# Neighbourhood attention on one core: 48 groups of four column blocks in three steps, with the weighted values of a group in one run

## The chip, the core and the metric

The kernel runs on one NeuronCore of a Trainium2 chip. A time is device microseconds of one execution of the whole program. Five engines have a part here: TensorE (PE in the profile, its weight loads PEld), VectorE (DVE), ScalarE (ACT), GpSimd (POOL) and SyncE (SP), which issues every DMA of the program on one queue. Each engine takes its instructions in the order in which they were written into its stream.

## What is computed

One layer of an encoder runs over 16 meta tokens, a batch of 512 tokens (p) and one of 1024 tokens (a and b, 512 each), all with the same weights, in float32. The input is normalised and projected to seven parts of 1024 columns: two for a gated convolution of width 31 and its gate, three for attention (q, k, v) and one for its gate. Attention has 16 heads of 64 and looks at a window of the token grid around each query. Cut to what matters here:

```
s = einsum('bjqhd,brjkhd->bhjqrk', q_r, k_blk) + bias + mask_add
s_meta = einsum('bjqhd,bmhd->bhjqm', q_r, k_meta_s)
p = softmax(concatenate([s, s_meta], axis=-1), axis=-1)
o = einsum('bhjqrk,brjkhd->bjqhd', p_grid, v_blk) + einsum('bhjqm,bmhd->bjqhd', p_meta, v_meta)
mixed = concatenate([conv_out, att * silu(a_gate)], axis=-1)
y = h + rms_norm(einsum('ble,ed->bld', mixed, w_out))
```

## The kernel before

A projection is made of 24 matmuls into one PSUM bank (`mm`, line 133): eight slices of the contraction, and for each the product of the rounded weights with the rounded input and two correction products with the rest of the weights (`wlo`) or of the input. The program runs in three stages. First come the norm and the convolution (on DVE), with projections of the gates and of v beside it; then attention; then the gated product with the output weights (`py`, line 682), for 12 tiles of 128 tokens.

Attention goes over 8 pairs of heads (`p`) and, for each, 3 ranges of the grid (`g`), which share one k projection (`pair_proj`, four projections) and have one q projection each (`pair_q`). A range has 8 column blocks of 64 queries. One column block takes these steps:

- scores: 3 matmuls into a bank of pool `ps_s`, which has two banks (`ss`, line 548);
- softmax: DVE adds the bias table and takes the maximum (line 556), ACT the exponential (559), DVE scales by the reciprocal of the sum (561); the tile is `pt`;
- transposes: 2 or 3 on PE into a bank of `ps_t`, which has two banks too (`tp`, line 564), and ACT copies them to `pT` (566);
- weighted values: 4 or 6 matmuls with 64 columns of weights (`po`, line 571). The two heads of a pair write partitions 0 to 63 and 64 to 127 of one bank, so these matmuls use half the columns of the array each; every other matmul of this stage uses all 128. The trace holds two records for each of these instructions.

After 8 column blocks DVE copies the bank out (`mo`, line 574), and SP writes it to memory (`mad`, 575). Nothing in the code says how these steps interleave: a list scheduler orders each engine's stream. It takes what is written first in the code before what is written later, where both are ready by its own estimate of times, and fills with later work where not. So the projections that are written for the next range or pair become fill between the steps of the current one.

At the end of attention the first tile of the output stage (`mix(0)`) is queued, on ACT, behind the last exponential. The output weights (`load_wo`, lines 616 to 627) are loaded by SP, rounded by ACT and split by DVE.

Of the kernel before, what the change touches and what calls it, by code (L numbers as in the profile page):

```python
# [53 lines left out]
VPB = 1  # L54

# [12 lines left out]
def tile_encoder(ctx: ExitStack, tc: tile.TileContext, mt, xn, w_main, w_v, wo, cw, cb, lg, lb, pg, postg, rbt, rmask, y):  # L68
# [25 lines left out]
    msq = const.tile([128, 128], F32, name="msq")  # L94
# [368 lines left out]

    def pair_proj(p):
# [3 lines left out]
        kl = pool.tile([128, 8, NROW, 8], F32R, name="kl")  # L468
        for (c0, c1) in MGROUPS:
# [34 lines left out]
    def pair_q(p, wqh, wql, g):  # L504
        ps = ps_mm.tile([128, 512], F32, name="mm", tag="mm")
        proj(ps, wqh, wql, 16 + g * 512, 16 + g * 512 + 512)
        res = []
        for hf in range(2):
# [8 lines left out]
            res.append((qh, ql))  # L517
        return res

    def attention(p, g, kh, kl, qs):  # L520
        G = GR[g]
        R = G["R"]
        R8 = R * 8
        esl = slice(p * 128, p * 128 + 128)
        if g == 0:
# [3 lines left out]
        else:  # L529
            vt = apool.tile([104, 8, 128], F32, name="vt", bufs=2)  # L530
            nc.sync.dma_start(vt[:R8], vd[:, G["vrow"] * 8:G["vrow"] * 8 + R8, esl].rearrange("b k e -> k b e"))
        po = ps_o.tile([128, 8, 64], F32, name="po")
        for j in range(8):
            qh, ql = qs[j // 4]
            jj = j % 4
            e = ebufs[g][{0: 1, 7: 2}.get(j, 0)]
            if g == 0:
                b0, nk, key = min(max(j - 1, 0), 5), 3, "k3"
            elif j in (0, 7):
                b0, nk, key = min(j, 6), 2, "k2"  # L540
            else:
                b0, nk, key = j - 1, 3, "k3"
            nt, kt = (2, 108) if g == 0 else (nk, R8)
            ra, rn, ro = G[key]
            w = rn * 8
            ss = ps_s.tile([128, 512], F32, name="ss")
            for i, (q, k) in enumerate(((qh, kh), (qh, kl), (ql, kh))):
                nc.tensor.matmul(ss[:, :nk * w], lhsT=q[:, jj].rearrange("p h x -> p (h x)"),  # L548
                                 rhs=k[:, b0:b0 + nk, ra:ra + rn, :].rearrange("p b r c -> p b (r c)"),
                                 start=(i == 0), stop=(i == 2))  # L550
# [3 lines left out]
            pv3 = pv.rearrange("p (k x) -> p k x", k=nk)  # L554
            sm = apool.tile([128, 4], F32, name="sm", bufs=4)
            nc.vector.tensor_tensor_reduce(out=pv3, in0=sv_, in1=e.rearrange("p k r c -> p k (r c)"), scale=1.0,  # L556
# [4 lines left out]
            nc.vector.tensor_scalar(out=pv, in0=pv, scalar1=sm[:, 3:4], scalar2=None, op0=ALU.mult)  # L561
            tp = ps_t.tile([128, 512], F32, name="tp")
# [3 lines left out]
            nc.scalar.copy(out=pT[:kt, :nt * 128], in_=tp[:kt, :nt * 128])  # L566
            for k in range(nt):
                for h in range(2):
                    hs = slice(h * 64, h * 64 + 64)
                    v = vt[:, k, b0, hs] if g == 0 else vt[:R8, b0 + k, hs]  # L570
                    nc.tensor.matmul(po[hs, j, :], lhsT=v, rhs=pT[:kt, k * 128 + h * 64:k * 128 + h * 64 + 64],  # L571
                                     start=(k == 0), stop=(k == nt - 1))
        mo = apool.tile([128, 512], F32, name="mo", bufs=2)
        nc.vector.tensor_copy(out=mo, in_=po.rearrange("p j x -> p (j x)"))
        nc.sync.dma_start(mad[g][p], mo)

    for p in range(NPAIR):
        e_build(p)
        kh, kl = pair_proj(p)
        wqh, wql = load_w(24 + p)  # L580
        for g in range(3):
            qs = pair_q(p, wqh, wql, g)
            attention(p, g, kh, kl, qs)
        if p >= NAG1:
            for _ in a_gate(p):
                pass
    for cs in [(c,) for c in range(NCG1, 6)] + [(6, 7)]:
        for _ in c_gate(cs):
            pass
# [192 lines left out]
```

## Time and profile before

| | before |
|---|---|
| time, median of 3 runs | 1517.15 us (1515.48 to 1517.2) |
| the profiled execution, its own time | 1517.83 us |
| its span, first to last instruction | 1516.1 us |
| around the span (1517.83 - 1516.1) | 1.73 us |
| PE busy | 1460.5 us (96%) |
| DVE, ACT, POOL busy | 1006.9, 585.3, 351.4 us |
| granted TensorE clock, mean | 0.986 |
| first scores to the last matmul of weighted values (starts) | 725.9 to 1234.8 us |

PE's busy time counts each matmul from its start to its end, and matmuls of a stream overlap, so it doesn't say how densely they follow one another. What a matmul costs the stream is the distance from its start to the start of the next one, read from the timeline. In the timeline, equal instructions that follow one another are one row, with a count (x16) and the length from the first start to the last end.

### The profile page before, as it was taken

The page shows a single profiled execution, that of the slowest core. Times are in us where ns is not written, and L with a number is a line of the kernel's source. Part 1 is how long each engine was busy: PE and PEld are TensorE (multiplying, and loading weights), DVE is VectorE, ACT ScalarE, POOL GpSimd, SP SyncE. Part 2 cuts the span into 40 slices and gives each one's busy share as a digit, 9 for nine tenths or more (in the row PEclk, how much of TensorE's full clock was granted, in tenths as well). Part 3 has the DMA queues.
Part 4 walks back from the last instruction along what each step waited for, and adds up shares of the span by engine and source line. Part 5 has one row for each costly group of instructions (what it writes and reads, how often), then busy time and mean ns, then how long its engine had stood idle before and what let it go on. Part 6 is the DMA issues. An engine that isn't in the chain of part 4 may idle for free.

```text
span 1516.1 us, 24156 instructions
## 1 busy us (share of the span) xinstructions
PE 1460.5 (96%) x9506; PEld 1241.3 (82%) x9506; DVE 1006.9 (66%) x1739; ACT 585.3 (39%) x1296; POOL 351.4 (23%) x258
## 2 busy tenths in 40 slices
PE   7998999999999898969999999999999979999998
PEld 6987898989988787757888888888887867888876
DVE  7699989797959698991545545546555557553442
ACT  7312121122111121112544545545544567456652
POOL 1133232233031323562121111111210002122121
PEclk9999999999999999989999999999999999999999
DMA  8013123141122131024112222212222367454542
GB/s 274 24 49 104 46 59 112 53 137 61 48 74 90 38 103 63 29 87 122 52 56 65 63 61 82 66 44 61 86 58 81 119 189 218 131 169 131 148 137 75
DMA packets 124470, 138.91 MB, mean 92 GB/s; under 512 B 8110, under 2 KB 96430, under 8 KB 124356
## 3 DMA queue, kind: packets, MB, share of 16 engines
q1 hardware_dynamic: 124356, 137.36, 29.6%
q8 instruction: 75, 1.23, 0.3%
q14 instruction: 39, 0.32, 0.1%
HBM read 99.05 MB, written 42.71 MB: 94 GB/s over the span
## 4 chain that ended last, share of the span: by engine, by line
PE 76%; DVE 9%; DMA 6%; issue 4%; POOL 2%; ACT 2%; SPq 0%; DVEq 0%; POOLq 0%; ACTq 0%
PE mm L133 49%; PE mm L286 8%; DVE z L223 5%; PE ss L548 5%; PE po L571 5%; PE tp L564 4%; PE py L682 4%; DMA mb<-std 2%; DMA mx<-zs 2%; POOL wlo L116 1%; POOL ml L655 1%; DMA yo<-in_wo 1%; DVE mx L653 1%; DVE mx L649 1%; DVE mx L648 1%
## 5 line engine op out<-in xcount | busy, mean ns | idle before, releaser
L133 PE MATMUL mm<-uw,whi 128*128 128x512 f32 (+2 forms) x2688 | 757.2, 364 | 3.2 <-ACT whi L115 3.2
L133 PEld LDWEIGHTS mm<-uw,whi 128*128 128x128 f32 x2688 | 485.1, 190 | 83.7 <-ACT whi L115 4.9
L223 DVE SCALAR_TENSOR_TENSOR z<-ub,cw_sb,z 128x1536 f32<-128x1536 f32 (+2 forms) x300 | 507.7, 1710 | 23.4 <-ACT z L221 15.2
L133 PE MATMUL mm<-uw,wlo 128*128 128x512 f32 (+2 forms) x1344 | 488.4, 364 | 18.1 <-POOL wlo L116 18.1
L133 PEld LDWEIGHTS mm<-uw,wlo 128*128 128x128 f32 x1344 | 255.6, 190 | 56.8 <-POOL wlo L116 19.1
L116 POOL TENSOR_TENSOR wlo<-wraw,whi 128x1024 fp32r<-128x1024 f32 x48 | 150.0, 3126 | 437.9 <-ACT whi L115 433.0
L682 PE MATMUL py<-uw,mh 128*128 128x512 f32 x576 | 180.0, 394 | 6.8 <-ACT mh L654 6.2
L286 PE MATMUL mm<-vh,uw 128*128 128x256 f32 x768 | 141.9, 284 | 1.1 <-ACT uw L158 0.6
L566 ACT COPY pT<-tp 108x256 f32<-108x256 f32 (+4 forms) x192 | 76.1, 425 | 153.4 <-PE tp L564 146.9
L682 PEld LDWEIGHTS py<-uw,mh 128*128 128x128 f32 x576 | 108.8, 189 | 31.1 <-ACT mh L654 6.4
L286 PEld LDWEIGHTS mm<-vh,uw 128*128 128x128 f32 x768 | 119.4, 190 | 3.3 <-ACT uw L158 1.0
L559 ACT ACTIVATE pt<-pt,sm 128x216 f32<-128x216 f32 (+4 forms) x192 | 96.9, 505 | 46.3 <-DVE sm L558 44.6
L682 PE MATMUL py<-uw,ml 128*128 128x512 f32 x288 | 113.2, 394 | 0.8 <-POOL ml L655 0.8
L556 DVE CUSTOM_DVE_ANT_0 pt<-ss,ei 128x216 f32<-128x216 f32 (+2 forms) x144 | 60.8, 439 | 77.7 <-PE ss L548 73.7
L655 POOL TENSOR_TENSOR ml<-mx,mh 128x1024 fp32r<-128x1024 f32 x22 | 54.4, 2490 | 245.5 <-ACT mh L654 245.5
L286 PE MATMUL mm<-vl,uw 128*128 128x256 f32 x384 | 108.1, 282 | 0.0
L561 DVE TENSOR_SCALAR pt<-pt,sm 128x216 f32<-128x216 f32 (+4 forms) x192 | 76.2, 397 | 5.5
L564 PE MATMUL tp<-ident,pt 128*96 128x128 f32 (+2 forms) x480 | 78.8, 282 | 0.0
L286 PEld LDWEIGHTS mm<-vl,uw 128*128 128x128 f32 x384 | 72.7, 189 | 0.8 <-issue 0.5
L115 ACT CAST whi<-wraw 128x1024 fp32r<-128x1024 f32 x48 | 50.3, 1048 | 48.9 <-PE mm L133 32.8
L571 PEld LDWEIGHTS po<-pT,vt 96*64 96x64 f32 (+1 forms) x1408 | 47.8, 137 | 23.5 <-issue 13.4
L682 PEld LDWEIGHTS py<-uw,ml 128*128 128x128 f32 x288 | 54.4, 189 | 13.6 <-POOL ml L655 1.3
(147 smaller groups left out, 1630.7 us busy)
## 6 DMA issues: line engine op xcount, KB each, us to landing
wraw<-in_w_main SPq DMA_DIRECT2D x48, 512.0 KB
xt<-in_xn SPq DMA_DIRECT2D x12, 512.0 KB
vd<-vs SPq DMA_DIRECT2D x96, 64.0 KB
zs<-zc SPq DMA_DIRECT2D x24, 256.0 KB
cgd<-ag SPq DMA_DIRECT2D x24, 256.0 KB
agd<-ag SPq DMA_DIRECT2D x24, 256.0 KB
mad<-mo SPq DMA_DIRECT2D x24, 256.0 KB
mx<-zs SPq DMA_DIRECT2D x12, 512.0 KB
```

The source lines that it names most:

```text
L116: eng.tensor_tensor(out=lo, in0=raw, in1=hi.bitcast(F32), op=ALU.subtract)
L133: nc.tensor.matmul(ps[:, :n], lhsT=w[:, dc, :], rhs=u[dc // 4][:, dc % 4, :], start=(dc == 0 and i == 0), stop=(dc == DC - 1 and i == 2))
L223: nc.vector.scalar_tensor_tensor(out=zv, in0=ub[:, a:b, k:k + 512], scalar=cw_sb[:, c, k:k + 1], in1=zv, op0=ALU.mult, op1=ALU.add)
L286: nc.tensor.matmul(ps[:, :256], lhsT=u[dc // 4][:, dc % 4, :], rhs=w[dc // 4][:, dc % 4, :], start=(dc == 0 and i == 0), stop=(dc == DC - ...
L548: nc.tensor.matmul(ss[:, :nk * w], lhsT=q[:, jj].rearrange("p h x -> p (h x)"), rhs=k[:, b0:b0 + nk, ra:ra + rn, :].rearrange("p b r c -> ...
L559: last[0] = nc.scalar.activation(out=pv, in_=pv, func=AF.Exp, bias=sm[:, 1:2], scale=1.0, accum_out=sm[:, 2:3])
L561: nc.vector.tensor_scalar(out=pv, in0=pv, scalar1=sm[:, 3:4], scalar2=None, op0=ALU.mult)
L564: nc.tensor.transpose(out=tp[:kt, k * 128:k * 128 + 128], in_=pv[:, k * kt:k * kt + kt], identity=ident)
L566: nc.scalar.copy(out=pT[:kt, :nt * 128], in_=tp[:kt, :nt * 128])
L571: nc.tensor.matmul(po[hs, j, :], lhsT=v, rhs=pT[:kt, k * 128 + h * 64:k * 128 + h * 64 + 64], start=(k == 0), stop=(k == nt - 1))
L655: (nc.vector if t < MLT else nc.gpsimd).tensor_tensor(out=ml, in0=mx, in1=mh.bitcast(F32), op=ALU.subtract)
L682: nc.tensor.matmul(pss[hf], lhsT=m[e // 8][:, e % 8], rhs=w[e][:, hf * 512:hf * 512 + 512], start=(e == 0 and i == 0), stop=(e == 15 and i ...
```

## The change

The steps of a column block are written apart, for groups of four column blocks: 8 pairs x 3 ranges x 2 halves make 48 groups. Step n of the loop writes the scores and softmax of group n, the weighted values of group n-2, the transposes of group n-1 and one unit of projections, in this order. The weighted values are queued on PE behind the last score matmul written so far (`issue_after`), and thereby stand together. There are now 6 `pt` tiles, 4 `pT` tiles, one `mo` tile and 2 `raw` tiles (3, 2, 2 and 3 before). The work of the last groups is followed by what is left of the gate projections, as before.

```diff
...
+PTB, PTTB = 6, 4
...
     def pair_proj(p):
...
+        kbufs[p] = kh, kl
...
-        return kh, kl
+            yield
...
-            raw = apool.tile([128, 15, 24], F32, name="raw", bufs=3)
+            raw = apool.tile([128, 15, 24], F32, name="raw", bufs=2)
...
+    def scores(p, g, hf):
+        if hf == 0:
+            load_values(p, g)
+        kh, kl = kbufs[p]
+        qh, ql = qbuf.pop((p, g, hf))
+        R8 = GR[g]["R"] * 8
+        for jj in range(4):
...
-            pt = apool.tile([128, 312], F32, name="pt", bufs=3)
+            pt = apool.tile([128, 312], F32, name="pt", bufs=PTB)
...
+    def transposes(p, g, hf):
+        for j in range(hf * 4, hf * 4 + 4):
...
             for k in range(nt):
                 nc.tensor.transpose(out=tp[:kt, k * 128:k * 128 + 128], in_=pv[:, k * kt:k * kt + kt], identity=ident)
-            pT = apool.tile([108, 384], F32, name="pT", bufs=2)
+            pT = apool.tile([108, 384], F32, name="pT", bufs=PTTB)
             nc.scalar.copy(out=pT[:kt, :nt * 128], in_=tp[:kt, :nt * 128])
...
+    def weighted(p, g, hf):
+        if hf == 0:
+            pos[p, g] = ps_o.tile([128, 8, 64], F32, name="po")
+        po, vt = pos[p, g], vts[p, g]
+        for j in range(hf * 4, hf * 4 + 4):
...
+    def between(p, i):
+
+        if i in (0, 2):
+            pair_q(p, i // 2 + 1)
+        elif p == NPAIR - 1:
+            next(rest, None)
+        elif i == 5:
+            pair_q(p + 1, 0)
+        else:
+            if i == 1:
+                knext[0] = pair_proj(p + 1)
+                next(knext[0])
+            next(knext[0])
...
+    groups = [(p, g, hf) for p in range(NPAIR) for g in range(3) for hf in range(2)]
+    for n in range(len(groups) + 2):
+        if n < len(groups):
+            p, g, hf = groups[n]
+            if (g, hf) == (0, 0) and p > 0:
+                e_build(p)
+            scores(p, g, hf)
+        else:
+            next(rest, None)
+        if n >= 2:
+            with tc.issue_after(last_qk[0].ins):
+                weighted(*groups[n - 2])
+        if 0 <= n - 1 < len(groups):
+            transposes(*groups[n - 1])
+        if n < len(groups):
+            between(p, g * 2 + hf)
```

What the scheduler makes of it, engine by engine, is read from the two built programs; lines 564, 586 and 602 of the changed kernel are the scores, transposes and weighted values. First PE in the middle of a pair, a range's last weighted values before the change:

```order
L133 MATMUL mm<-uw,whi 128x512 x2
L571 MATMUL po<-pT,vp 64x64 x8
L564 MATMUL tp<-ident,pt 108x128 x4
L548 MATMUL ss<-kh,qh_5536 128x264
L548 MATMUL ss<-kl,qh_5536 128x264
L548 MATMUL ss<-kh,ql_5537 128x264
```

PE at such a place after the change:

```order
L133 MATMUL mm<-uw,whi 128x512 x2
L586 MATMUL tp<-ident,pt 108x128 x2
L564 MATMUL ss<-kh,qh_5535 128x264
L564 MATMUL ss<-kl,qh_5535 128x264
L564 MATMUL ss<-kh,ql_5536 128x264
L602 MATMUL po<-pT,vt 64x64 x22
L564 MATMUL ss<-kh,qh_5541 128x256
```

The weighted values of two column blocks stood between projections and transposes; those of four now stand between scores, and the transposes stand apart from them in twos and threes. Over the whole stage, counted in the two orders, the 960 weighted-value instructions make 120 runs before and 50 after; behind a run stand transposes 107 times before (33 after), scores 10 times (16) and others 3 times (1). The 480 transposes make 133 runs before and 208 after; 21 and 92 of them have a projection right behind. Behind the last scores of the stage PE still has 31 projection matmuls, 22 weighted-value instructions and 5 transposes before, and 33, 66 and 18 after.

Second, PE where one pair of heads follows another, before the change:

```order
L571 MATMUL po<-pT,vt 64x64 x6
L564 MATMUL tp<-ident,pt 104x128 x2
L548 MATMUL ss<-kh,qh_5530 128x264
L548 MATMUL ss<-kl,qh_5530 128x264
L548 MATMUL ss<-kh,ql_5531 128x264
L571 MATMUL po<-pT,vt 64x64 x6
L564 MATMUL tp<-ident,pt 108x128 x2
L548 MATMUL ss<-kh,qh_5536 128x264
```

PE at this place after the change; the first row is a score matmul of the old pair's last group, the rows with `qh_5529` belong to the new pair:

```order
L564 MATMUL ss<-kh,ql_5542 128x312
L586 MATMUL tp<-ident,pt 104x128
L564 MATMUL ss<-kh,qh_5541 128x256
L564 MATMUL ss<-kl,qh_5541 128x256
L564 MATMUL ss<-kh,ql_5542 128x256
L602 MATMUL po<-pT,vt 64x64 x22
L586 MATMUL tp<-ident,pt 104x128 x4
L133 MATMUL mm<-uw,whi 128x256
L586 MATMUL tp<-ident,pt 104x128 x3
L564 MATMUL ss<-kh,qh_5529 128x264
```

The old pair's last two column blocks, a whole run of weighted values and seven transposes now stand in front of the new pair's first scores, with one projection matmul among them. And DVE at this place after the change (`ql` and `kl` are the rests of the rounded q and k, ISA is line 556's addition and maximum, line 571 here):

```order
L522 SCALAR_TENSOR_TENSOR ql_5542<-mm,qh_5541 64x4x64
L482 TENSOR_TENSOR kl<-mm,kh 128x8x8
L522 SCALAR_TENSOR_TENSOR ql_5542<-mm,qh_5541 64x4x64
L482 TENSOR_TENSOR kl<-mm,kh 128x8x8
L606 COPY mo<-po 128x512
L571 ISA pt,sm<-ss,ei_5563 128x312
L571 ISA sm 128x1
L571 ISA pt,sm<-ss,e_5565 128x208
```

DVE at this place before:

```order
L479 TENSOR_TENSOR kl<-mm,kh 128x8x8
L560 RECIPROCAL sm<-sm 128x1
L556 ISA pt,sm<-ss,ei_5548 128x216
L556 ISA sm 128x1
L561 TENSOR_SCALAR pt<-pt,sm 128x216
L558 TENSOR_SCALAR sm<-sm 128x1
L479 TENSOR_TENSOR kl<-mm,kh 128x8x8
```

The four rests and the copy of `mo` now stand in a row, ahead of the additions that empty the two score banks; before, additions stood between them.

## Rows read from the trace of the kernel before

**Rows 1.** Windows: us, busy PE, PEld, DVE, ACT, POOL, PEclk, DMA share, GB/s.

```profile
726.00:1224.00 498.00, 497.40 (x4314) 419.74 (x4313) 272.07 (x1122) 251.56 (x736) 70.71 (x79) 1.00 0.24 72
1224.00:1241.00 17.00, 9.31 (x80) 7.26 (x78) 7.79 (x14) 15.12 (x25) 0.00 (x0) 0.90 0.31 86
```

**Rows 2.** Chain of waits from 726 to 1230 us, shares by line.

```profile
by line: PE mm L133 55.9%; PE ss L548 15.3%; PE po L571 14.4%; PE tp L564 13.2%; ACT gt L652 0.4%; ACT L639 0.3%; ACT L652 0.3%; ACT pt L559 0.1%; issue 0.1%; ACT pT L566 0.1%; DVE pt L556 0.1%; DVE sm L558 0.0%; ACT mb L639 0.0%; DVEq L556
```

**Rows 3.** Waits of TensorE (PE) and its weight loads (PEld), 726 to 1230 us.

```profile
PE po L571 <- ACT pT L566: 0.6, 1, 0.6
...
PEld po L571 <- issue: 19.6, 61, 0.4
```

**Rows 4.** Timeline, TensorE, one cycle: start, length, line, operation, shape, count.

```profile
932.75 0.61 PE L133 MATMUL mm<-uw,whi 128*128 128x512 f32 x2
933.20 0.39 PE L133 MATMUL mm<-uw,wlo 128*128 128x512 f32 x1
933.52 0.69 PE L571 MATMUL po<-pT,vp 108*64 108x64 f32 x16
934.13 0.65 PE L564 MATMUL tp<-ident,pt 128*108 128x128 f32 x4
934.54 0.38 PE L548 MATMUL ss<-kh,qh 128*128 128x288 f32 x1
```

**Rows 5.** Timeline, TensorE: the shortest and the longest run of weighted values.

```profile
739.90 0.45 PE L571 MATMUL po<-pT,vp 108*64 108x64 f32 x8
740.29 0.43 PE L564 MATMUL tp<-ident,pt 128*108 128x128 f32 x2
...
950.53 0.92 PE L571 MATMUL po<-pT,vt 96*64 96x64 f32 x24
951.38 0.86 PE L564 MATMUL tp<-ident,pt 128*96 128x128 f32 x6
```

**Rows 6.** Timeline, TensorE, where transposes stand alone and scores follow weighted values.

```profile
1216.48 0.49 PE L564 MATMUL tp<-ident,pt 128*104 128x128 f32 x3
1216.73 0.48 PE L133 MATMUL mm<-uw,whi 128*128 128x512 f32 x1
1217.14 0.80 PE L571 MATMUL po<-pT,vt 104*64 104x64 f32 x20
1217.87 0.41 PE L548 MATMUL ss<-kh,qh 128*128 128x312 f32 x1
1218.12 0.30 PE L548 MATMUL ss<-kl,qh 128*128 128x312 f32 x1
...
1218.55 0.30 PE L548 MATMUL ss<-kl,qh 128*128 128x312 f32 x1
1218.69 0.49 PE L564 MATMUL tp<-ident,pt 128*104 128x128 f32 x3
1218.94 0.39 PE L548 MATMUL ss<-kh,ql 128*128 128x312 f32 x1
1219.16 0.39 PE L133 MATMUL mm<-uw,wlo 128*128 128x512 f32 x1
```

**Rows 7.** Costliest groups, VectorE: busy us and mean ns; then one timeline row.

```profile
L515 DVE SCALAR_TENSOR_TENSOR ql<-mm,qh 64x256 fp32r<-64x256 f32 x96 | 40.2, 419 | 19.7 <-ACT qh L514 18.8
L574 DVE COPY mo<-po 128x512 f32<-128x512 f32 x24 | 16.5, 687 | 16.2 <-PE po L571 16.0
L556 DVE CUSTOM_DVE_ANT_0 pt<-ss,ei 128x312 f32<-128x312 f32 x48 | 22.1, 481 | 30.8 <-PE ss L548 29.9 <-PE tp L564 0.8
...
854.11 0.22 DVE L479 TENSOR_TENSOR kl<-mm,kh 128x64 fp32r<-128x64 f32 x1
```

**Rows 8.** Timeline, the end of attention: TensorE, then the DMA queue of SP.

```profile
1241.26 2.08 PE L682 MATMUL py<-uw,mh 128*128 128x512 f32 x4 [6.25 <-ACT mh L654]
...
1240.72 0.38 SPq L575 DMA_DIRECT2D mad<-mo  x1
1241.19 0.41 SPq L616 DMA_DIRECT2D xr<-in_wo  x1
```

More of the change, by code (lines that the diff above doesn't have):

```diff
@@ L93, in tile_encoder @@
     sel = const.tile([128, 16], F32, name="sel")
-    msq = const.tile([128, 128], F32, name="msq")
     cw_sb = const.tile([128, DC, KW], F32, name="cw_sb")
@@ L462, in tile_encoder @@
     last = [None]
+    kbufs = {}
     def pair_proj(p):
@@ L516, in pair_q, with block, load_values @@
                                                in1=qh[hs, :, h, :].bitcast(F32), op0=ALU.mult, op1=ALU.subtract)
[L517 to L523, printed above, removed]
+            qbuf[p, g, hf] = qh, ql
+    vts, pts, pTs, pos = {}, {}, {}, {}
+    def block(g, j):
+        e = ebufs[g][{0: 1, 7: 2}.get(j, 0)]
+        if g == 0:
+            return min(max(j - 1, 0), 5), 3, "k3", 2, 108, e
+        R8 = GR[g]["R"] * 8
+        if j in (0, 7):
+            return min(j, 6), 2, "k2", 2, R8, e
+        return j - 1, 3, "k3", 3, R8, e
+    def load_values(p, g):
         esl = slice(p * 128, p * 128 + 128)
+        R8 = GR[g]["R"] * 8
         if g == 0:
@@ L530, in attention @@
             vt = apool.tile([104, 8, 128], F32, name="vt", bufs=2)
[L531 to L544, printed above, removed]
+            nc.sync.dma_start(vt[:R8], vd[:, GR[g]["vrow"] * 8:GR[g]["vrow"] * 8 + R8, esl].rearrange("b k e -> k b e"))
+        vts[p, g] = vt
+    def scores(p, g, hf):
[3 more added lines that the diff above has]
+        qh, ql = qbuf.pop((p, g, hf))
+        R8 = GR[g]["R"] * 8
+        for jj in range(4):
+            j = hf * 4 + jj
+            b0, nk, key, _, _, e = block(g, j)
+            ra, rn, ro = GR[g][key]
             w = rn * 8
@@ L561, in attention @@
             nc.vector.tensor_scalar(out=pv, in0=pv, scalar1=sm[:, 3:4], scalar2=None, op0=ALU.mult)
+            pts[p, g, j] = pv
+    def transposes(p, g, hf):
+        for j in range(hf * 4, hf * 4 + 4):
+            _, _, _, nt, kt, _ = block(g, j)
+            pv = pts.pop((p, g, j))
             tp = ps_t.tile([128, 512], F32, name="tp")
@@ L575, in attention @@
[L575 to L589, printed above, removed]
+        if hf == 1:
+            mo = apool.tile([128, 512], F32, name="mo", bufs=1)
+            nc.vector.tensor_copy(out=mo, in_=pos.pop((p, g)).rearrange("p j x -> p (j x)"))
+            nc.sync.dma_start(mad[g][p], mo)
@@ new lines, in last_gates @@
+    def last_gates():
+        for p in range(NAG1, NPAIR):
+            yield from a_gate(p)
+        for cs in [(c,) for c in range(NCG1, 6)] + [(6, 7)]:
+            yield from c_gate(cs)
+    rest = last_gates()
+    def between(p, i):
[10 more added lines that the diff above has]
+            next(knext[0])
@@ new lines, in tile_encoder @@
+    knext = [None]
+    e_build(0)
+    for _ in pair_proj(0):
+        pass
+    pair_q(0, 0)
+    groups = [(p, g, hf) for p in range(NPAIR) for g in range(3) for hf in range(2)]
[14 more added lines that the diff above has]
+            between(p, g * 2 + hf)
@@ L590, in tile_encoder @@
+    for _ in rest:
+        pass
     es2.close()
@@ L600, in tile_encoder @@
     mb = mp1.tile([128, 2, 128], F32, name="mb")
+    msq = mp1.tile([128, 128], F32, name="msq")
     mp2 = ctx.enter_context(tc.tile_pool(name="mp2", bufs=1, side="right", reuse_waits="tile"))
```

24 lines of the change are left out of this document (14 added, 10 removed).

## Prediction

> **What bounds the kernel now.** I read the windows of the attention stage first, because the change touches nothing before it. From 726 to 1224 us PE is busy for 497.40 of 498.00 us at a granted clock of 1.00, DVE for 272.07 and ACT for 251.56 [rows 1]. Next the chain of waits: PE's four kinds of matmul make 55.9 + 15.3 + 14.4 + 13.2 = 98.8% of what set the end of this stage [rows 2]. Then the table of waits: in 504 us PE waited once for another engine, 0.6 us [rows 3]. So the stage is bound by PE's stream, and the question is not whether PE waits but what its stream costs. The same table has an oddity: 61 times, 19.6 us in all, the weight loads sat idle in front of a weighted-values matmul until "issue", that is with nothing to wait for [rows 3]. Something is lost where the stream turns to the half-width matmuls. The timeline says how much.
>
> **The price of one run of weighted values.** All from starts.
> - Into the run: two 512-column projection matmuls take 933.20 - 932.75 = 0.45 us, 0.23 each; the last one before the run takes 933.52 - 933.20 = 0.32 [rows 4]. Entry costs 0.09.
> - The run: 8 records take 740.29 - 739.90 = 0.39 us, 24 take 951.38 - 950.53 = 0.85 [rows 5]. That is 0.46 / 16 = 0.029 per record and 0.39 - 8 x 0.029 = 0.16 per run; 16 records, 934.13 - 933.52 = 0.61 [rows 4], leave 0.15. I take 0.15.
> - Out of it: 3 transposes without such a run in front take 1216.73 - 1216.48 = 0.25, so 4 would take 0.25 + 0.11 = 0.36; behind a run 4 take 934.54 - 934.13 = 0.41 [rows 4, 6]. With transposes behind, exit costs 0.05. With scores behind, the first takes 1218.12 - 1217.87 = 0.25 where a later one takes 1218.69 - 1218.55 = 0.14 [rows 6]: 0.11.
>
> A run costs 0.24 us beyond its records, and 0.05 or 0.11 for what follows. [...]
>
> **The change, part by part.**
> - Removed: 70 of 120 runs (counted in the two orders). Before: 120 x 0.24 + 107 x 0.05 + 12 x 0.11 = 35.5 us. After: 50 x 0.24 + 33 x 0.05 + 16 x 0.11 = 15.4. Saved: 20.1 us. PE is the bound there, so all of it is on the path.
> - Moved: the transposes, from 133 runs to 208. Among scores, 3 transposes and the next score take 1219.16 - 1218.69 = 0.47, as much as 0.25 + 0.08 for three in a row plus 0.14 for a score: free. In front of a projection, 1217.14 - 1216.48 = 0.66, against 0.33 + 0.23 + 0.09 (the entry into the run behind) = 0.65 [rows 6]: 0.01 each, 71 more such places, 0.7 us. No DMA, copy or DVE work is added; all of that stage's instructions are the same ones.
> - Added, waits of PE. Before there is 0.6 us of them; the trace cannot show those of another order, so I bound them. The place that worries me is the change from one pair to the next, seven times. There the new pair's first scores need the score bank of the column block before last, which DVE empties only behind `ql`, `kl`, `ql`, `kl` and `mo` in its stream. `mo` needs the end of the weighted-values run. PE meanwhile has 7 transposes and one 256-column projection matmul, about 7 x 0.11 + 0.12 + 0.05 = 0.9 us. DVE needs 0.69 for `mo` and 0.48 for the addition after that run [rows 7], 1.2 us and two handovers, so PE falls 0.3 us or more behind. If the rests are late too, since they wait for ACT, add 0.42 + 0.22 + 0.42 + 0.22 = 1.28 [rows 7], in all about 1.6. A second wait, for ACT's copies out of the two transpose banks, can stand beside it. I take 1.0 per change, 7 us; bounds 0 and 2 x 7 = 14. At the other group changes 20 or more projection matmuls (some 5 us) lie in between and cover such a chain; queued behind a late PE are only DVE and ACT, which are half idle there.
> - Moved at the end: behind the last scores PE has 44 more weighted-value instructions (88 records), 13 more transposes and 2 more projection matmuls: 88 x 0.029 + 13 x 0.11 + 2 x 0.23 + three more runs at 0.29 = 5.3 us. That is no new work, but it lies later. PE idles there, 6.25 us before the first product of the output stage [rows 8], 17.00 - 9.31 = 7.7 us in the window from 1224 on [rows 1], and one could hope that it fills the hole. I don't think so: SP's queue writes the last `mad` (1240.72) just in front of the last eight loads of output weights (`xr` at 1241.19) [rows 8], and that write waits for the last weighted values. Later weighted values make later weights, and PE then waits for these instead. I charge 2 us for it: ACT has four `pT` copies more behind the last exponential. Bounds: -4 (the hole is filled) and +5 (the weights come that much later).
>
> Sum against the profiled execution's 1517.83: -20.1 + 0.7 + 7 + 2 = -10.4, so 1507.4. That execution lies 0.68 us above the median of 1517.15, so against the runs shown it is 1506.7. Forecast: **1507 us**. A difference of 0.2%, 3 us, is about what a measurement of this kernel can tell from none: faster is under 1514.1, slower over 1520.2.
>
> **The rivals.**
> - *The new waits stay hidden.* The change at a pair costs nothing and the end neither. For it: DVE is busy 55% of the time, and PE waited for nothing before. Against: the row of five DVE instructions ahead of the additions. -20.1 + 0.7 = -19.4, some 1498 us.
> - *The saving is eaten.* Waits reach their upper bounds, 14 in the stage and 5 at the end: -20.1 + 0.7 + 19 = -0.4, some 1517 us, within 0.2%. For it: the scheduler places transposes and scores by its own estimate of times, closer to one another than before, so that small errors now show. [...]
> - *Slower: ACT blocks.* There are four `pT` tiles, one group's worth. ACT's copy of the next group's first transposes must wait for the weighted values that free a tile, and those now stand behind the last scores of a still later group. If a PE that runs late makes ACT stop at that copy, the exponentials behind it in ACT's stream stop too, then the softmax, the `pt` tiles, the scores. It decides from 48 groups x 0.40 us = 19.4, that is from 0.4 us per group on. If each group lost as much as the one wait for ACT of before, 0.6 [rows 3]: 48 x 0.6 = 29, so -19.4 + 29 + 2 = +12, some 1529 us. Against it: ACT is half idle, and two transpose banks let PE run two column blocks ahead.
> - *The change does nothing,* the order being left to the scheduler: excluded by the order, which has 50 runs.
>
> **How the numbers follow.** The forecast's case, 1502 to 1513 us with waits between 4 and 15 us: 0.64. Hidden waits, 1496 to 1502: 0.13. Eaten, 1513 to 1520: 0.15, of which 0.02 still count as faster. Slower: 0.08. So faster 0.79, same 0.13, slower 0.08. The range leaves out half of the hidden case's lower end and the slower case, and a little of the eaten one: 1499 to 1516.
>
> **What the next profile would show.** Right: the distance from a projection matmul to a run still 0.32, 50 runs of 32 or 44 records (44 in 44 x 0.029 + 0.15 = 1.43 us) in place of 120; the "issue" idle of weight loads in front of `po` down from 61 times to almost none, since most runs now follow scores of under 0.15 us; the last scores some 18 us earlier (20.1 - 0.7 - 7 and the 5.3 that moved behind them), the first product of the output stage 12 to 16 us earlier, and waits for output weights inside its first tile that give 2 to 6 us of it back; PE waits of about 1 us at each of seven pair changes. Wrong: a run's fixed part growing with its length, transposes costing when they stand alone, waits spread over all groups, or an output stage more than 9 us longer than before.

## The result and the profile after

The changed kernel takes 1506.79 us (median of 4 runs, 1506.1 to 1508.56) against 1517.02 for the kernel before on the same chip: ratio 0.9937, 95% interval [0.9919, 0.9954]. That is 10.2 us faster; 1507 was forecast, in a range of 1499 to 1516. The profiled execution took 1506.1 us with a span of 1504.3, so 11.7 and 11.8 less than that of before. Lines have moved: scores are L564 now, transposes L586, weighted values L602, `pT` copies L588, output products L747.

The windows answer to [rows 1]; columns: us, busy time of PE, PEld, DVE, ACT, POOL with counts, granted clock, DMA share, GB/s.

```profile
725.00:1203.00 478.00, 476.89 (x4227) 414.60 (x4227) 278.83 (x1119) 255.08 (x728) 70.74 (x79) 1.00 0.25 73
1203.00:1220.00 17.00, 14.85 (x176) 11.68 (x173) 7.11 (x16) 15.49 (x30) 0.00 (x0) 1.00 0.21 67
1220.00:1252.00 32.00, 23.54 (x80) 16.22 (x81) 22.60 (x19) 20.81 (x27) 5.27 (x2) 0.87 0.95 298
1252.00:1504.00 252.00, 246.11 (x1074) 201.87 (x1072) 107.10 (x152) 140.25 (x227) 48.26 (x20) 0.99 0.45 133
```

Up to the last scores (now at 1202.3) PE is still the bound: 476.89 of 478 us. The new hole is the third window, where PE works 23.54 of 32 us while the DMA engines are at 95%. That is the first tile of the output stage. The hole of before lay ahead of it [rows 1, 8].

The table of waits from 725 to 1222 us answers to [rows 3]; columns: total us, times, longest.

```profile
PEld po L602 <- issue: 3.1, 18, 0.2
...
PEld ss L564 <- DVE sm L571: 1.8, 4, 0.4
...
PE tp L586 <- ACT pT L588: 1.2, 1, 1.2
PE po L602 <- ACT pT L588: 0.9, 1, 0.9
PE ss L564 <- DVE sm L571: 0.8, 4, 0.2
```

The idle of weight loads until "issue" fell from 19.6 us in 61 places to 3.1 in 18. New are waits for score banks, four of them, with 0.2 us each in PE's rows, and two waits for `pT` behind the last scores.

The four stand where one pair of heads follows another. The first of them in the timelines of TensorE and of VectorE:

```profile
900.74 0.36 PE L133 MATMUL mm<-uw,whi 128*128 128x256 f32 x1
901.17 0.54 PE L586 MATMUL tp<-ident,pt 128*104 128x128 f32 x3
901.90 0.39 PE L564 MATMUL ss<-kh,qh 128*128 128x264 f32 x1 [0.20 <-DVE sm L571]
...
900.17 0.43 DVE L522 SCALAR_TENSOR_TENSOR ql<-mm,qh 64x256 fp32r<-64x256 f32 x1 [0.32 <-ACT qh L521]
900.63 0.23 DVE L482 TENSOR_TENSOR kl<-mm,kh 128x64 fp32r<-128x64 f32 x1
900.77 0.68 DVE L606 COPY mo<-po 128x512 f32<-128x512 f32 x1
901.37 0.47 DVE L571 CUSTOM_DVE_ANT_0 pt<-ss,ei 128x312 f32<-128x312 f32 x1
```

By starts such a place costs more than the 0.2 us of the row. The three transposes ahead of the scores take 901.90 - 901.17 = 0.73 us in place of 0.25 [rows 6], and the projection matmul in front of them about 0.2 more than usual, since the next weight load waits 0.3 us for ACT's copy out of a transpose bank. That is some 0.7 us for each, 3 us for the four.

The timeline of TensorE shows one run; it answers to [rows 4, 5].

```profile
967.00 0.28 PE L564 MATMUL ss<-kh,ql 128*128 128x264 f32 x1
967.21 1.50 PE L602 MATMUL po<-pT,vt 104*64 104x64 f32 x44
968.64 0.54 PE L586 MATMUL tp<-ident,pt 128*104 128x128 f32 x3
```

A score whose step is 0.124 us elsewhere takes 0.21, so entry costs 0.09 as before, and 44 records take 1.43 us, what the prediction worked out.

The timeline at the end, TensorE first and then SP's queue, answers to [rows 8].

```profile
1229.87 0.40 PE L747 MATMUL py<-uw,ml 128*128 128x512 f32 x1
1232.22 0.73 PE L747 MATMUL py<-uw,mh 128*128 128x512 f32 x2 [1.96 <-ACT uw L691]
1233.48 0.72 PE L747 MATMUL py<-uw,mh 128*128 128x512 f32 x1 [0.53 <-DVE uw L692]
1234.00 0.63 PE L747 MATMUL py<-uw,ml 128*128 128x512 f32 x1
1234.42 0.63 PE L747 MATMUL py<-uw,mh 128*128 128x512 f32 x1
1234.85 0.63 PE L747 MATMUL py<-uw,ml 128*128 128x512 f32 x1
...
1251.23 0.80 PE L747 MATMUL py<-wlo,mh 128*128 128x512 f32 x1 [3.43 <-DVE wlo L692]
...
1220.68 0.33 SPq L607 DMA_DIRECT2D mad<-mo  x1
1222.74 0.37 SPq L710 DMA_DIRECT2D mx<-mad  x1
1223.17 0.57 SPq L711 DMA_DIRECT2D gt<-agd  x1
1223.79 1.19 SPq L681 DMA_DIRECT2D xr<-in_wo  x1
```

The first `py` starts at 1219.8, behind the last weighted values without a pause, and then PE waits seven times, 8.4 us in all, for casts and splits (`uw`, `wlo`) of output weights. Their loads follow the last `mad` write on SP, as the prediction feared.

**Where the 11.7 us come from.** For every kernel below I summed the steps between starts of PE's records. *Price*: what the step into a run, the step out of it (beyond 0.0295 of a record) and the step of the first instruction behind it exceed the usual steps (0.229 for 512 columns, 0.109 for a transpose, 0.120 to 0.145 for a score; in e3 a record is 0.112). *Late*: what `py` steps longer than 0.45 us exceed 0.2305. Runs are counted in the order on PE. The ratio is that to the kernel before on the same chip, whose median was 1515.87 to 1517.32 in these comparisons. The runs come from several chips, so two of them are best compared by their ratios; places in the stream are from one profiled execution of each.

| kernel | runs | price | first py | late | last py | median | ratio to before, 95% |
|---|---|---|---|---|---|---|---|
| before | 120 | 31.5 | 1241.3 | 3.3 | 1509.2 | 1517.02 | |
| changed | 50 | 12.5 | 1219.8 | 11.5 | 1497.7 | 1506.79 | 0.9937 [0.9919, 0.9954] |
| e1_split2 | 87 | 25.2 | 1227.9 | 7.3 | 1500.6 | 1509.17 | 0.9953 [0.9939, 0.9966] |
| e2_buffers_alone | 107 | 27.8 | 1232.3 | 8.1 | 1507.8 | 1515.16 | 0.9990 [0.9981, 0.9999] |
| e3_full_width | 50 | 0.0 | 1253.5 | 10.8 | 1531.3 | 1539.79 | 1.0154 [1.0140, 1.0167] |
| e4_raw_on_top | 50 | 12.6 | 1225.8 | 6.5 | 1496.5 | 1504.19 | 0.9916 [0.9901, 0.9930] |
| e5_hold_mix | 50 | 12.6 | 1222.9 | 7.2 | 1495.9 | 1504.27 | 0.9914 [0.9901, 0.9927] |
| e6_weights_early | 50 | 13.9 | 1225.9 | 3.3 | 1494.5 | 1502.72 | 0.9906 [0.9893, 0.9919] |
| e7_third_score_bank | 52 | 13.7 | 1237.7 | 11.0 | 1515.4 | 1527.88 | 1.0061 [1.0043, 1.0080] |
| e8_no_order | 104 | 30.6 | 1242.3 | 0.8 | 1506.5 | 1515.58 | 0.9992 [0.9983, 1.0001] |
| e9_no_late_weights | 50 | 12.4 | 1221.1 | 4.1 | 1488.8 | 1498.13 | 0.9879 [0.9863, 0.9894] |
| e10_mo_on_act | 50 | 13.3 | 1221.9 | 10.9 | 1501.5 | 1511.06 | 0.9962 [0.9949, 0.9975] |
| e11_tail_spread | 51 | 13.0 | 1225.4 | 3.2 | 1492.4 | 1499.39 | 0.9883 [0.9870, 0.9897] |
| e12_before_no_late_weights | 120 | 31.2 | 1239.5 | 0.4 | 1504.0 | 1514.05 | 0.9978 [0.9969, 0.9988] |

From before to the changed kernel: price -19.0; the pause ahead of the first `py`, 6.4, gone; transposes and waits in the attention stage +4.7 (what is left over when the other terms are taken off; some 3 of it are the four pair changes); first scores 0.8 earlier. Together the first `py` comes 21.5 us earlier. From there to the last `py` it is 277.9 us in place of 267.9: 10.0 given back, of which 8.2 is *late*; another 1.6 lies in `py` steps between 0.30 and 0.45 us, which exceed the usual by 3.1 us in place of 1.5. 21.5 - 10.0 = 11.5, the distance of the last `py`.

### The profile page after: what moved, and what is told of

Read it like the earlier page. It is cut to its first block, busy times and chain, and to the rows that moved or that the text cites. A ratio compares the mean times of both kernels' runs of the same rounds, so it can differ in the third digit from the quotient of the medians.

```text
span 1504.3 us, 24024 instructions
## 1 busy us (share of the span) xinstructions
PE 1448.5 (96%) x9506; PEld 1241.5 (83%) x9506; DVE 1011.4 (67%) x1739; ACT 597.2 (40%) x1300; POOL 349.0 (23%) x258
## 4 chain that ended last, share of the span: by engine, by line
PE 88%; DVE 7%; DMA 2%; ACT 1%; POOL 1%; issue 1%; SPq 0%; DVEq 0%; ACTq 0%; POOLq 0%
PE mm L133 49%; PE py L747 16%; PE mm L286 8%; DVE z L223 5%; PE ss L564 5%; PE po L602 4%; PE tp L586 3%; POOL wlo L116 1%; DMA xr<-in_wo 1%; DMA gb<-in_pg 0%; PE ss L423 0%; PE ss L155 0%; PE tp L155 0%; PE ss L233 0%; DMA mb<-std 0%
## 5 line engine op out<-in xcount | busy, mean ns | idle before, releaser
L133 PE MATMUL mm<-uw,wlo 128*128 128x512 f32 (+2 forms) x1344 | 490.4, 365 | 18.1 <-POOL wlo L116 18.1
L747 PE MATMUL py<-uw,mh 128*128 128x512 f32 x576 | 181.8, 396 | 5.0 <-ACT uw L691 2.7
L747 PEld LDWEIGHTS py<-uw,mh 128*128 128x128 f32 x576 | 109.1, 190 | 31.5 <-DVE uw L692 4.3
L747 PE MATMUL py<-uw,ml 128*128 128x512 f32 x288 | 113.7, 395 | 0.0
L588 ACT COPY pT<-tp 108x256 f32<-108x256 f32 (+4 forms) x192 | 79.4, 424 | 62.9 <-PE tp L586 52.8
L586 PE MATMUL tp<-ident,pt 128*96 128x128 f32 (+2 forms) x480 | 87.7, 275 | 1.5 <-ACT pT L588 1.2
L576 DVE RECIPROCAL sm<-sm 128x1 f32<-128x1 f32 x192 | 31.3, 163 | 71.9 <-ACT pt L575 69.4
L586 PEld LDWEIGHTS tp<-ident,pt 128*96 128x96 f32 (+2 forms) x480 | 56.9, 128 | 16.2 <-ACT pT L588 2.8
L713 DVE TENSOR_TENSOR mx<-mx,mb 128x1024 f32<-128x1024 f32 x12 | 16.8, 1400 | 78.8 <-DMA mx<-zs 78.8
```

Source lines behind the costliest of these rows:

```text
L133: nc.tensor.matmul(ps[:, :n], lhsT=w[:, dc, :], rhs=u[dc // 4][:, dc % 4, :], start=(dc == 0 and i == 0), stop=(dc == DC - 1 and i == 2))
L747: nc.tensor.matmul(pss[hf], lhsT=m[e // 8][:, e % 8], rhs=w[e][:, hf * 512:hf * 512 + 512], start=(e == 0 and i == 0), stop=(e == 15 and i ...
```

## Experiments

**Theory**: each run has a fixed price, and what it saves is partly given back to late output weights. **Rival**: buffers and the longer pipeline bring the gain.

**e1, two runs where there was one.**

```diff
...
-        if n >= 2:
-            with tc.issue_after(last_qk[0].ins):
-                weighted(*groups[n - 2])
-        if 0 <= n - 1 < len(groups):
-            transposes(*groups[n - 1])
+        for js in ((0, 1), (2, 3)):
+            if n >= 2:
+                with tc.issue_after(last_qk[0].ins):
+                    weighted(*groups[n - 2], js)
+            if 0 <= n - 1 < len(groups):
+                transposes(*groups[n - 1], js)
```

> The changed kernel, with the weighted values of each group issued as two pieces of two column blocks, with two column blocks of transposes between the pieces; every buffer and all arithmetic as in the changed kernel. Its order on PE has 87 runs of weighted values in place of 50, the same matmuls. Theory (each run costs a fixed price of 0.29 us beyond its records): 37 x 0.29 = 10.7 us more than the changed kernel, about 1517.5 us, with the same 0.3 us from the matmul before a run to its second record's start. Rival (the gain comes from the deeper buffers and from the one step more between softmax, transposes and weighted values, not from fewer runs): no more than 2 us from the changed kernel, 1505 to 1509.

The timeline of TensorE, at a place where the changed kernel has one run of 44:

```profile
910.19 0.28 PE L564 MATMUL ss<-kh,ql 128*128 128x264 f32 x1
910.40 0.92 PE L602 MATMUL po<-pT,vt 104*64 104x64 f32 x24
911.25 0.32 PE L586 MATMUL tp<-ident,pt 128*108 128x128 f32 x1
911.50 0.80 PE L602 MATMUL po<-pT,vt 104*64 104x64 f32 x20
912.23 0.39 PE L133 MATMUL mm<-uw,wlo 128*128 128x256 f32 x1
```

Both pieces and the transpose take 912.23 - 910.40 = 1.83 us; one run of 44 and a transpose take 1.43 + 0.11 = 1.54. The price is 0.29 for one run more, as forecast. Over the kernel it rises by 12.7 us, 0.34 for each of 37 runs, and the first `py` comes 8.1 later. Yet the time rises by 2.4 only (medians; 0.9953 against 0.9937, intervals that overlap). Of the 8.1 the output stage gave 5.2 back (272.7 us in place of 277.9), since the weights are less late. The stream's 12.7 arrive as 8.1 in part because the four waits at pair changes, some 3 us, are absent in this order: its table of waits has no wait for a score bank. So I was wrong on the time and right on the stream. The time alone doesn't exclude the rival's 1505 to 1509, but the rival has no room for the 12.7 us in the stream.

**e2, the buffers alone**, in the kernel before:

```diff
...
-            pt = apool.tile([128, 312], F32, name="pt", bufs=3)
+            pt = apool.tile([128, 312], F32, name="pt", bufs=6)
...
-            pT = apool.tile([108, 384], F32, name="pT", bufs=2)
+            pT = apool.tile([108, 384], F32, name="pT", bufs=4)
...
```

> The kernel before, with only the buffers of the changed kernel (six pt, eight sm, four pT, two raw, one mo, msq moved): weighted values of a column block still follow its transposes. Its order on PE has 107 runs in place of 120. Theory (price per run): 13 x 0.29 = 3.8 us less than the kernel before, about 1513 us. Rival (the buffers bring the gain): about 1507 us, as the changed kernel.

1515.16, 0.7 us below before on the same chip (1515.87). The rival's 1507 is excluded, and my 1513 is missed as well. The price fell by 3.7, as 13 runs should; the first `py` came 9.0 earlier, 3.3 of it because the pause ahead of it shrank to 3.1, and 7.6 was given back in the output stage (275.5 us).

**e3, the same runs in full width.**

```diff
...
-                for h in range(2):
-                    hs = slice(h * 64, h * 64 + 64)
-                    v = vt[:, k, b0, hs] if g == 0 else vt[:kt, b0 + k, hs]
-                    nc.tensor.matmul(po[hs, j, :], lhsT=v, rhs=pT[:kt, k * 128 + h * 64:k * 128 + h * 64 + 64],
+                v = vt[:, k, b0, :] if g == 0 else vt[:kt, b0 + k, :]
+                nc.tensor.matmul(po[:, j % 4, :], lhsT=v, rhs=pT[:kt, k * 128:k * 128 + 128],
...
```

> The changed kernel, with the weighted values of a column block and key block made by one matmul of all 128 columns of the values tile and all 128 query columns (both heads; the two cross blocks are computed and not copied out) in place of two with 64 columns and 64 rows of the output each; the output tile holds four column blocks of 128 columns, and DVE copies the two blocks that are wanted, two copies of 64 x 256 behind each run in place of one of 128 x 512 behind every second. 50 runs as before. Theory (the fixed price is that of turning PE from 128-column matmuls to half-width ones and back): the 50 prices of 0.29 to 0.35 us go, 15 us, and 480 matmuls of 128 columns at the 0.109 us of a transpose take the place of 1920 records at 0.029, 52.3 for 55.7, 3.4 us less; DVE has 17 us more to do and may add 1 to 3 us of waits: 1488 to 1492 us. In its trace the distance from a score to the first matmul of a run and from there to the second is that of any other matmul. Rival (the price belongs to the start of a run in any width, such as a weight load that is not hidden): only the 3.4 us, 1503 to 1505.

```profile
964.42 0.31 PE L564 MATMUL ss<-kh,ql 128*128 128x312 f32 x1
964.57 2.62 PE L600 MATMUL po<-pT,vt 96*128 96x128 f32 x22
966.94 0.39 PE L564 MATMUL ss<-kh,qh 128*128 128x312 f32 x1
967.17 0.30 PE L564 MATMUL ss<-kl,qh 128*128 128x312 f32 x1
```

That timeline holds both my hit and my miss. The score ahead of the run takes 0.15, its usual step: entry, 4.4 us in the changed kernel, is 0.2 here. The run and the score behind it take 967.17 - 964.57 = 2.60, which is 22 x 0.112 for the records and 0.14 for a score. That first score has 0.23, but the last record in front of it only 0.03 (from the starts of single records), so nothing is lost between them. The whole price is 0.0 us within what these sums can tell, in place of 12.5. So the price belongs to the turn between full-width and half-width matmuls. What PE does in such a turn the trace does not show. But I priced the wide matmul wrong: it has two records of 0.112 us, where I had counted one of 0.109. Inside the runs the 960 records cost 45.9 us more than the 1920 half-width ones, and the last records of the 50 runs 50 x (0.112 - 0.0295) = 4.1 more. 45.9 + 4.1 - 12.5 leaves 37.5; without the pair changes' 3 us, which are absent here as in e1, some 34.5. The first `py` came 33.7 later, and the kernel became 33.0 slower. This version without the turn doesn't pay.

**e8, grouped but without the issue order.**

```diff
-            with tc.issue_after(last_qk[0].ins):
-                weighted(*groups[n - 2])
+            weighted(*groups[n - 2])
```

> The changed kernel without the rule that a group's weighted values are issued behind the newest scores; groups, steps and buffers as in the changed kernel. Its order has 104 runs of weighted values in place of 50, and 117 runs of transposes in place of 208. Theory (price per run, 0.34 us as e1_split2 measured it): 54 x 0.34 = 18.4 us more in PE's stream up to the first py, of which the output stage gives back 5 to 8 us since its weights then are there: 1516 to 1520 us. Rival (grouping and buffers bring the gain, the order is worth little): 1506 to 1509 us.

1515.58 us, within half a microsecond of the theory's lower end; the price rose by 18.1 for 54 runs, 0.34 each. The first `py` came 22.5 later than in the changed kernel, and the output stage gave 13.6 of that back (264.3 us). The rule on issuing is what makes the 50 runs. Without it groups and buffers are worth 1.1 us (0.9992 [0.9983, 1.0001]), no difference clear of noise.

**e9 and e12, no late weights.** Both kernels got this edit:

```diff
-        load_wo(e)
+        if e in (6, 7) or e > 9:
+            woh.append(woh[e % 6])
+            wol.append(wol[e % 6])
+        else:
+            load_wo(e)
```

> The changed kernel without the last eight loads of output weights (rows 6, 7 and 10 to 15) and their casts and subtractions: their products use the tiles of rows 0 to 5 again, so eight of sixteen weight rows are left out of the result. PE's work is the same. Theory (half of what the attention stage won is given back while the first output tile waits for late weights): the waits inside that tile, 11.5 us in the changed kernel, fall under 2, and the time by 9 to 11 us: 1496 to 1498 us, some 20 below the kernel before. Rival (the output stage is slow for another reason, such as the mix of the second tile): above 1502 us.

> The kernel before with the edit of e9_no_late_weights: rows 6, 7 and 10 to 15 of the output weights are not loaded, cast or split, and their products use the tiles of rows 0 to 5; eight of sixteen rows are left out of the result. Compared with e9 it shows what the changed attention is worth where no late weight can take it back. Theory: before the edit the kernel's first output tile waits only 3.3 us, so it wins 1 to 4 us by it, 1513 to 1516, and lies 15 to 18 us above e9 (1498.1); the kernels as they are lie 10 apart. Rival (the weights cost both kernels the same): 1508 us, 10 above e9.

The changed kernel gains 8.7 us by it, 1498.13, just above the forecast; the kernel before 3.3 (1514.05 against 1517.32). Without late weights the two lie 15.9 us apart, in place of 10.2; by the ratios, since the chips differ, 15.0 in place of 9.6. So the attention is worth 15 to 16 us, of which 5 to 6 are lost to the weights. The rival's 10 is excluded. *Late* fell to 4.1 in e9 and not under 2: what is left there are waits for the mix (`mh`, `ml`), 3.5 us, and none for weights. The edit takes away the loads together with their casts and subtractions, so it doesn't tell which of these came late.

**e4 to e6 and e11, the end of attention.** In the changed kernel's memory `mx2` begins 320 bytes ahead of the end of `mo` (`msq`, moved, pushed it there). That is my reading of the layout; the trace shows only that SP waited 1.7 us for the landing of `mad` in front of the load of `mx`. e4 and e5:

```diff
...
-            raw = apool.tile([128, 15, 24], F32, name="raw", bufs=2)
+            raw = rpool.tile([128, 15, 24], F32, name="raw", bufs=2)
...
-            mix(1)
+            with tc.issue_after(last_pT[0].ins):
+                mix(1)
```

> The changed kernel, with the two raw tiles in a pool of their own behind the attention pool, so that they lie at the upper end of its memory, and the 320 bytes of mo that the second mix tile overlaps become bytes of a raw tile, free long before. Same order of instructions on PE. Theory (the tail loses its time to this overlap: SP holds the load of the second mix tile until the last mad write has landed, 1220.68 to 1222.74, and the output-weight loads stand behind it): that load issues right behind the mad write, the weight loads start 1.7 us earlier, and the first output tile waits 1.5 to 2 us less: 1505 us. Rival (the loads are bound by what frees xr, yo and wraw or by the transfers themselves): no change, 1506 to 1507.5.

> The kernel of the run before this with raw on top (e4_raw_on_top), with ScalarE's instructions of the second output tile's mix kept behind the last copy of a transpose bank; nothing else moves on PE. In e4 PE stood 5.2 us in front of the last weighted values, since ACT had that mix (a table load, a root, two gates, a cast) ahead of the last two pT copies. Theory (what is won behind the last scores is lost again to ACT's order): the wait of 5.2 us falls under 1 us, the first py comes 4 to 5 us earlier than in e4, the weights of output rows then come late instead, and 1 to 4 us of it are left: 1500 to 1503 us. Rival (the output stage is bound by the arrival of the weights alone, so that an earlier first py only waits longer inside its first tile): 1504 us as e4.

e4 (the first of the two edits) comes close to the time that I named, for another reason. Its first weight load of the tail went out later, at 1228.73, not earlier; behind the last `mad` write it came 2.07 us, in place of 3.11 in the changed kernel. The order of ACT had changed, and PE stood for it; ACT's timeline, then PE's:

```profile
1216.91 0.83 ACT L589 COPY pT<-tp 104x384 f32<-104x384 f32 x2
1218.64 1.28 ACT L705 ACT_TABLE_LOAD   x1 [0.90 <-DMA mb<-std]
...
1224.03 0.75 ACT L589 COPY pT<-tp 104x384 f32<-104x384 f32 x2
...
1224.56 1.33 PE L603 MATMUL po<-pT,vt 104*64 104x64 f32 x20 [5.24 <-ACT pT L589]
```

The first `py` came 6.0 later than in the changed kernel, and the last one 1.2 earlier. e5 took part of that wait away: first `py` 2.9 earlier, time the same, 1504.27. The rival's time is right here: an earlier start was given back inside. Its *late* rose by 0.7 only, so part of the 2.9 I cannot place.

e6 adds to e5 what brings weights earlier, and e11 spreads ACT's work (the lines with `g == 2` and with 12, 13, 8 and 9) and drops the second edit of e5:

```diff
...
-        pool = apool if p % 2 else kpool
+        pool = kodd if p % 2 else kpool
...
-        nc.sync.dma_start(raw, wo[e])
+        (nc.gpsimd if e in (6, 7) else nc.sync).dma_start(raw, wo[e])
...
+    WORD = (0, 1, 2, 3, 4, 5, 8, 9, 12, 13, 6, 7, 10, 11, 14, 15)
...
-    for e in range(16):
+    for e in WORD:
...
+            if p == NPAIR - 1 and g == 2:
+                nc.vector.tensor_copy(out=pT[:kt, :nt * 128], in_=tp[:kt, :nt * 128])
...
+        if e in (12, 13):
+            with tc.issue_after(pool_load[0].ins):
+                nc.gpsimd.tensor_copy(out=h, in_=raw)
+        else:
+            (nc.vector.tensor_copy if e in (8, 9) else nc.scalar.copy)(out=h, in_=raw)
...
```

> e5_hold_mix, with three edits that bring output weights earlier: kh and kl of odd pairs lie with raw at the upper end of the attention pool, so that the staging tiles xr and yo overlap what the last scores free and not what the last weighted values free; the loads of rows 6 and 7 go through GpSimd's queue instead of standing behind the last mad write on SP's; and the rows staged in wraw (8, 9, 12, 13) are loaded and used ahead of 6, 7, 10, 11 in the first output tile. Same sums in another order of rows. Theory (the time given back at the end is waiting for weights): 10 rows are there when the first py starts, 13.8 us of work, two more arrive behind GpSimd's loads at about 1205, and the waits inside the first output tile, 11.5 us in the changed kernel and 6.5 in e4, fall under 3: 1495 to 1500 us. Rival (the transfers themselves are the bound from 1224 to 1254, where the DMA engines are busy 70 to 90%): not below 1502.

> e6_weights_early, with ScalarE relieved behind the last scores: the last eight pT copies and the casts of weight rows 8 and 9 go to VectorE, those of rows 12 and 13 to GpSimd behind its two loads, and the second tile's mix is not held. In e6 ACT was busy almost without a gap from 1203 to 1224, and PE stood 6.9 us for its pT copies before the first py. Theory (in e6 the bound at this place is ACT's stream): these waits fall under 3 us, the first py starts 3 to 4 us earlier, the waits inside the first output tile stay at 3: 1497 to 1500 us. Rival (VectorE's stream, in which the copies now stand behind the same mix, holds them as long, or the first py waits for mh on ACT): 1502 to 1504.

In e6 *late* fell to 3.3, where I had said under 3, but the first `py` came at 1225.9, 6.1 later than in the changed kernel, for `pT` copies behind casts on ACT; 1502.72 misses my range and agrees with the rival's number, though the rival left no room for the fall of *late*. e11 moved those copies to DVE. The tables of waits from 1200 to 1226, of e6 and then of e11:

```profile
PE po L604 <- ACT pT L590: 3.2, 1, 3.2
PE tp L588 <- ACT pT L590: 1.9, 1, 1.9
```

```profile
PE po L607 <- DVE pT L591: 2.8, 2, 2.1
PE tp L588 <- DVE pT L591: 2.6, 1, 2.6
```

The wait changed its engine and kept its size, 5.1 and 5.4 us, as the rival said. The time fell nonetheless, to 1499.39: the output stage took 267.0 us in place of 268.6 and began 0.5 earlier, so the last `py` comes 2.1 earlier. The time lies in my range, but not for the reason that I named. e11 beats both kernels: 17.4 us below before on the same chip, 7.4 below the changed kernel's median.

**e7 and e10, the pair changes.**

```diff
-BMM, BSS, BTP = 3, 2, 2
+BMM, BSS, BTP = 2, 3, 2
```

```diff
-            nc.vector.tensor_copy(out=mo, in_=pos.pop((p, g)).rearrange("p j x -> p (j x)"))
+            (nc.scalar.copy if g == 2 else nc.vector.tensor_copy)(out=mo, in_=pos.pop((p, g)).rearrange("p j x -> p (j x)"))
```

> The changed kernel with three PSUM banks for scores and two for projections in place of two and three; 52 runs of weighted values in its order in place of 50. Theory (PE's waits at the pair changes are for a score bank that DVE has not emptied): the four waits of about 0.9 us in front of scores go, 3 to 4 us: 1503 to 1504. Rival (a projection bank is missed as much as a score bank is gained, since a copy out of a bank for 512 columns takes DVE and ACT 0.6 us and more): 1506 to 1510, with waits of projection matmuls for ACT or DVE in the table of waits.

> The changed kernel, with the copy mo of the third output row group of each pair, the one that stands at a pair change, made by ScalarE in place of VectorE. 50 runs as before. Theory (at a pair change DVE reaches the addition that empties the score bank late because mo, 0.69 us, stands in front of it): the four waits of 0.9 us fall to 0.3 or less each, 2 to 3 us: 1504 to 1505 us. Rival (the chain is held by ACT's rests and casts as well, so that mo only moves the wait): 1506 to 1508 us, with the same waits of PE in front of scores.

My 0.9 for each was too much: it is 0.7 by starts, 0.48 of it in front of the scores. e10 missed what it was meant to test. The weighted values run two groups behind the scores, so the copy that stands ahead of the addition at a pair change is that of the second range (`g == 1`); the edit moved that of the third. DVE and PE in e10 at the place shown above for the changed kernel:

```profile
899.46 0.68 DVE L606 COPY mo<-po 128x512 f32<-128x512 f32 x1
...
900.60 0.39 PE L564 MATMUL ss<-kh,qh 128*128 128x264 f32 x1 [0.20 <-DVE sm L571]
```

So the row of waits stayed the same, 0.8 us in 4 places, and whether `mo` holds the bank was not tested. The kernel became 4.3 slower, 2.1 of it before the first `py`; 1511.06 misses both ranges. With a third score bank one such wait of 0.3 is left, and from first scores to first `py` it takes 492.7 us in place of 494.4; but the first scores came 19.6 us later, and 1527.88 misses both ranges. (Its nine times spread from 1515.91 to 1530.45; the trace is of one of 1523.7.) Ahead of them PE lacked a projection bank, in the table of waits up to 745 us:

```profile
PE mm L133 <- ACT vs L272: 16.4, 2, 15.7
```

## Why the prediction was right, point by point

- **Price of a run, 20.1 us saved.** Right: 19.0 by the sum over starts. Both of its parts were too large, 31.5 and 12.5 where I had 35.5 and 15.4: a run cost 0.26 us before and 0.25 after, not 0.30 and 0.31, and in the difference most of that error drops out. e1, e2 and e8, which change the number of runs alone or nearly so, give 0.34, 0.29 and 0.34 for a run, against 0.24 + 0.05 = 0.29 and 0.24 + 0.11 = 0.35 taken from single rows.
- **Transposes in more runs, 0.7, and waits at pair changes, 7.** Too large: 4.7 for both with the two waits at the end. Four of seven pair changes wait, some 0.7 us each and not 1.0. The chain that I added up is the one that stands there in the trace: `ql`, `kl`, `mo` and the addition without a pause on DVE, and PE's score starts at 901.90, when the addition is done; beside it stands the wait for a transpose bank. That a score bank is what PE misses is shown by e7, where one such wait, of 0.3 us, is left of four. What `mo` alone is worth is not shown, since e10 moved another copy.
- **The end, 2 us, bounds -4 and +5.** The net is right: -6.4 for the pause and +10.0 inside, +3.6. Its parts are not what I said. The first `py` came 21.5 us earlier, not 12 to 16, because the pause did close; and the output stage is 10.0 us longer, past the 9 that I had set as a sign of a wrong prediction. That sign did come, and what stands behind it is that the first tile starts earlier than its weights, 8.2 us, and runs at a lower clock, 0.87 granted from 1220 to 1252 us in place of 0.95 from 1241 to 1273 us in the kernel before. Both errors cancel in the sum of 1507; without late weights the change is worth 15 to 16 (e9, e12), between my sum and the rival with hidden waits.
- **The sum.** Against the forecast the three terms are off by +1.1, -3.0 and +1.6 us, and the first scores, for which I had no term, came 0.8 earlier. That 1507 was met so closely is luck; that fewer runs save some 19 us, and that a good part of it is given back behind them, is not.
- **The rivals.** *Hidden waits* (1498) lies nearer to the stage, where the pair changes cost 3 us, than my 7, and fails at the end. *Eaten* is excluded by the ratio. *ACT blocks* is absent in the stage, where no PE wait for `pT` is listed before 1203 and weight loads wait for such copies only 1.1 us, at the four pair changes, and present behind the last scores, 2.1 us here and 5.2 in e4.

What stays open: how much of the four waits at pair changes goes when the right copy of `mo` is moved; whether the weights are late for their place in SP's queue, for their staging tiles (SP waited 9.8 us in 7 places for DVE to free one, from 1195 to 1260 us) or for the transfers themselves, with the DMA engines at 95%; and how much of the tail is left to win. In no run that uses all sixteen rows of weights did the first `py` start at 1220 with them in time.

## What to carry to other kernels

Where TensorE is the bound, count how often its stream turns between full-width and half-width matmuls, price a turn from the starts of records (0.25 to 0.34 us for a run here), and gather the half-width ones; but do not replace them by full-width ones without pricing these from their own rows (e3 became 33.0 us slower). Before promising the gain, ask what the next stage needs: an earlier start is worth only as much as its inputs are earlier, and 5 to 6 of 15 to 16 us were lost here to weights that came late. When buffers are moved, look at which tiles of the next stage they now overlap, and at the order of the engine that must empty the last banks.

## What the runs showed of the hardware

- Half-width records start in pairs: in the run at 967.21 us of the changed kernel the two of a pair start 0.007 us apart, and the next pair 0.051 later, 0.0295 for a record (from the starts of single records). A full-width record took 0.112 (e3). So 44 records and the way out of the run take 1.43 us, 22 full-width records for as many key blocks 22 x 0.112 = 2.46. At half of 0.112, four half-width records one after another would need 0.22 us, an estimate; they take 4 x 0.0295 = 0.12. That the two of a pair run side by side in the array is my reading of this; the trace does not show it. Half of the wide result is thrown away, and that is nearly what it costs.
- A run of half-width matmuls between full-width ones costs 0.25 to 0.34 us beyond its records; 50 runs of full-width ones in the same places cost 0.0 in all (e3).
- PE's clock fell behind waits in the output stage. From 1220 to 1252 us it was granted 0.87. Behind the two waits of 1.96 and 0.53 us the steps were 1234.42 - 1234.00 = 0.42 us, nearly twice the usual 0.23, at a granted clock of 0.50. The windows read 0.50 in three stretches, behind the waits for `pT` at the end of attention, behind these two, and behind the 3.43 us for `wlo`:

```profile
1220.00:1223.00 3.00, 3.00 (x7) 1.92 (x8) 1.79 (x2) 1.69 (x2) 0.00 (x0) 0.50 0.55 200
1234.00:1237.00 3.00, 2.45 (x7) 1.44 (x5) 3.00 (x4) 2.10 (x3) 0.00 (x0) 0.50 0.94 291
1251.00:1254.00 3.00, 2.77 (x7) 2.19 (x8) 3.00 (x4) 2.97 (x4) 0.00 (x0) 0.50 1.18 293
```

In e9, whose *late* is 4.1 in place of 11.5, the windows read 1.00 for nearly the same stretch:

```profile
1221.00:1252.00 31.00, 27.51 (x120) 21.23 (x116) 11.80 (x13) 15.79 (x22) 5.37 (x2) 1.00 0.71 211
```

So the output stage lost more than its late steps: 10.0 us were given back, and *late* grew by 8.2. Whether a wait lowers the clock, and which, is not shown: e9 too waited for `pT` before its first `py`, up to 1.9 us at once, and kept 1.00.
